# Attention in a planned order, with seven products for the queries and keys of two groups

## The chip, the cores and the metric

The kernel runs on one core of a Trainium2 chip. A core has a matrix engine (TensorE, PE in the profile, with its weight loads as PEld), three engines for elementwise work (VectorE or DVE, ScalarE or ACT, GpSimd or POOL), a queue that issues loads (SyncE or SP) and 16 DMA engines. The on-chip memory has 128 partitions; TensorE writes its sums into eight banks of a second memory, PSUM. The metric is the device time of one execution in microseconds (us).

## The reference, cut to what matters

Two transformer layers over 512 tokens of width 1024, all in float32. Layer 0 mixes the tokens with a gated recurrence, layer 1 with attention; each is followed by a gated feed-forward of width 2816. A conditioning vector gives, through a large matrix (`ada_w`), six vectors per layer that scale, shift and gate. The change lies mostly in the attention of layer 1:

```python
proj = (u @ w_in).reshape(B, S, N_GROUPS, 3, ATT_HEADS, ATT_HEAD_DIM)     # 512 x (3 groups x 3 x 8 heads x 128)
for gi, (window, dilation) in enumerate(((128, 1), (512, 4), (2048, 16))):
    q = apply_partial_rope(proj[:, :, gi, 0], cos, sin) * scale
    k = apply_partial_rope(proj[:, :, gi, 1], cos, sin)
    v = proj[:, :, gi, 2]
    o_g, lse_g = dilated_group_attention(q, k, v, window, dilation)
wts = softmax(stack(lses), axis=0)
o = einsum('gbsh,gbshd->bshd', wts, stack(outs))
y = o.reshape(B, S, D_MODEL) @ w_out
```

So there are 24 query/key pairs (8 heads in 3 groups), each a 1024 x 256 matrix against the 512 tokens.

## The kernel before, in words

**Three products for one.** To keep float32 precision, every operand of a matrix product is split into a high part (a copy on ScalarE into a reduced type) and a low part (the difference, a subtraction on VectorE). A product is then three matmuls: high by high, high by low, low by high (`three`, lines 437 to 440). One block of 128 output columns over a depth of 1024 is 8 x 3 = 24 matmuls with 512 tokens streaming (`block`).

**Seven products for eight.** In the feed-forwards' first products and in the values of groups 2 and 3 a 2 x 2 split of both matrices (Strassen's scheme, in Winograd's form) is used: seven half-size products take the place of eight, at the price of sums of the operands and of the results (`seven_products`, matmuls at line 853; `seven_values`, lines 1383 to 1466). The sums of the tokens' quarters are made once (`token_sums`, lines 748 to 770), the sums of the weights' quarters for each weight piece, in place in the raw buffer, and some of the products' sums by copying one PSUM bank into another as its start.

**Weights as a stream.** `Stream` (lines 38 to 135) holds one list of items in order of use: weight pieces of 1 MB ("w"), pieces for the seven products ("quarters", "half"), pieces of the conditioning matrix ("ada"), its closing steps ("do", "rows"). Two raw buffers alternate; the SyncE queue fills them. `take` hands out split pieces and, with a lead of two, has the next ones split in advance: line 88 copies the high part, line 89 subtracts the low part (whole pieces of 2048 columns), lines 108 and 109 do it in halves. There are three buffers for split pieces. A conditioning piece is four multiply-adds on VectorE (lines 257, 259); after two of them GpSimd sums over partitions (line 261), and small steps on VectorE turn the row into columns or add it to a gate (lines 271, 306).

**Attention.** The normalised tokens are copied into the order of the dilated groups (`apart`, lines 1676 and 1677). After the values of group 1 a loop runs over `order`: pairs of query and key, with the seven-product values of groups 2 and 3 for heads 0 to 3 near the start and for heads 4 to 7 in the middle. Each pair is two blocks of 24 matmuls, evacuated by ScalarE (lines 1704, 1705), with the rotary part turned on VectorE and copied back on ScalarE (lines 1712 to 1722). After each block `fl.tick()` lets one step of an earlier head follow: scores with masks and maxima (lines 1743 to 1775), the weights between groups (`merge_r`, `merge_n`: lines 1782 to 1805), transposes (1810 to 1817) and the sums over values (1836 to 1849). In this loop the build's scheduler sets the order on each engine. Everywhere that `tc.manual_schedule` stands, the order in the code is kept on TensorE, ScalarE, VectorE and GpSimd.

**After the loop.** `mixer_out` multiplies the eight heads' outputs by the output weights, one head per step `kt`, in manual order; the last steps of heads 6 and 7 stand between them in `tail`. Heads' outputs are split by `cut` (lines 434, 435), three of them first. Weights are taken at the first and the fifth step:

```python
for kt in range(3):
    cut(kt)
for kt in range(KT):
    if kt % 4 == 0:
        w = st.take(0)
    ...
    for t in range(NT):
        prods(y0[t], t, kt, w)
```

**The feed-forward of layer 0, second product.** Eleven weight pieces, each for two blocks of 128 of the inner width; `part` splits these blocks (lines 434, 435) two ahead. Conditioning pieces for layer 1 are woven between the weight pieces.

Of the kernel before, what the change touches and what calls it, by code (L numbers as in the profile page):

```python
# [1 line left out]

# [13 lines left out]
P = 128  # L16
# [21 lines left out]
class Stream:  # L38
# [73 lines left out]
    def whole(self):  # L112

        assert self.items[self.done][0] in WHOLE
        self.fill()
        self.done += 1
        return self.raw.pop(self.done - 1)
# [10 lines left out]
    def take(self, ahead=None):  # L128
# [7 lines left out]
        return self.ready.pop(0)  # L136

# [21 lines left out]
def block_kernel(tc, x, c, positions, ada_w, ada_b, norm_g, hgrn_w_in, lower, hgrn_norm_g, hgrn_w_out,  # L159
# [8 lines left out]
    with ExitStack() as ctx:  # L168
# [95 lines left out]
        def ada_item(l, v, hf, kq):  # L264
            src = ada_w[l, kq * 512:(kq + 1) * 512, v * D + hf * 512:v * D + (hf + 1) * 512]
            return ("ada", src.rearrange("(k p) n -> p k n", p=P), ada_chunk(l, v, hf, kq))
# [43 lines left out]
        def fin_item(l, v, hf):  # L310
            if v not in (2, 5):
                return ("do", None, col_fin(l, v, hf))
# [3 lines left out]
            return ("rows", (b, n), row_fin(l, v, hf))  # L316
# [62 lines left out]
        items += weave(f0b[:9], ada_seq((1, 1), (1, 0)), 0, 0.9) + f0b[9:]  # L379
# [4 lines left out]

        def aqk(g, hd):
            return ("w", tuple(AW[:, (g * 3 + k) * D + hd * P:(g * 3 + k) * D + (hd + 1) * P].rearrange(
                "(k p) n -> p k n", p=P) for k in range(2)))
# [23 lines left out]
        late = ada_seq((1, 2), (1, 4), (1, 3))  # L411
# [3 lines left out]
        woven(late[:8], 1.5)  # L415
# [4 lines left out]
        woven(late[8:], 1.3)  # L420
# [16 lines left out]
        def three(ps, ah, al, bh, bl, start, stop):  # L437
            pe.matmul(ps, ah, bh, start=start, stop=False)  # L438
            pe.matmul(ps, ah, bl, start=False, stop=False)  # L439
            pe.matmul(ps, al, bh, start=False, stop=stop)  # L440
# [942 lines left out]
        def seven_values(dsts, apart, th, tl):  # L1383


            C = lambda raw, c: V4(raw)[:, :, c * 256:c * 256 + 256]
            G = lambda t, o: V4(t[:, o * 1024:(o + 1) * 1024])
            u_of = lambda r, c: lambda kt, n: [a[:, r * 4 + kt, c * 256 + n * P:c * 256 + (n + 1) * P] for a in apart]
            t_of = lambda i: lambda kt, n: [a[:, i, kt, n * P:(n + 1) * P] for a in (th, tl)]
            raws, tiles = {}, {}  # L1390

            def cut(i, tile, o, k, c):
                hi, lo = tiles[i, tile]
                src = C(raws[i][k], c)
                act.copy(G(hi, o), src)
                dve.tensor_sub(G(lo, o), src, G(hi, o).bitcast(F32))

            def place(i, tile):
                tiles[i, tile] = st.part_tiles(V0)

            def prepare(i, step):
                if i >= len(dsts):
                    return
                if step == 0:
                    raws[i] = [st.whole(), st.whole()]
                    place(i, 0)
                    cut(i, 0, 0, 0, 0)
                    cut(i, 0, 1, 1, 1)
                elif step == 1:
                    place(i, 1)  # L1410
                    cut(i, 1, 0, 1, 0)
                    a, b = raws[i]
                    dve.tensor_add(C(b, 1), C(b, 1), C(a, 1))
                    dve.tensor_add(C(a, 1), C(a, 1), C(a, 0))
                    dve.tensor_add(C(a, 0), C(a, 0), C(b, 1))
                    dve.tensor_add(C(b, 0), C(b, 0), C(a, 0))
                    cut(i, 1, 1, 0, 0)
                elif step == 2:
                    place(i, 2)
                    cut(i, 2, 1, 0, 1)  # L1420
                    st.fill(1)
                    cut(i, 2, 0, 1, 1)
                else:
                    place(i, 3)
                    cut(i, 3, 0, 1, 0)
                    raws.pop(i)
                    st.fill()

            def run(ps, i, tile, o, us):
                hi, lo = tiles[i, tile]  # L1430
                for n in range(2):
                    for kt in range(4):
                        w = slice(o * 1024 + kt * 256, o * 1024 + (kt + 1) * 256)
                        three(ps[:, n * 256:(n + 1) * 256], *us(kt, n), hi[:, w], lo[:, w], kt == 0, kt == 3)

            H2 = lambda a: a.rearrange("p (n c) -> p n c", n=2)
            for step in range(3):
                prepare(0, step)
            for i, dst in enumerate(dsts):
                X, Y, Z, U = (dst[:, t:t + 2, c:c + 256] for c in (0, 256) for t in (0, 2))  # L1440
                m1 = bank("mm")
                run(m1, i, 0, 0, u_of(0, 0))
                act.copy(X, H2(m1))
                m4 = bank("a")
                run(m4, i, 0, 1, t_of(2))
                prepare(i, 3)
                m2 = bank("mm")
# [404 lines left out]
        for kind, g, i in order:  # L1852
            if kind == "v":
                if g == 1:

                    for fn in fl.at.pop(fl.n, []):
                        fn()
# [17 lines left out]
            for k in range(2):  # L1875
                ps = block(whi, wlo, k * D, P, u=apart)
                heads[i]["qk"[k], g] = qk_evac(ps, g, k, pair)
                if k == 1:
                    turn_pair(g, pair)
# [39 lines left out]
```

## Time and profile before

| what | value |
|---|---|
| median of 3 runs | 1510.54 us (1510.5 to 1513.27) |
| the profiled execution | 1511.44 us, span 1509.4 us |
| granted TensorE clock, mean | 0.997 |
| TensorE busy | 1493.7 us, 99% |
| VectorE busy | 1040.2 us, 69% |
| ScalarE busy | 746.6 us, 49% |
| GpSimd busy | 199.0 us, 13% |
| HBM | 192.31 MB read, 131 GB/s over the span |

The span is the time from the first to the last instruction that the profiler recorded; the execution's own time has some 2 us around it. Busy times are unions of an engine's instructions; matmuls overlap in their pipelines, so TensorE's progress is read better from the distance between the starts of matmuls than from the duration of one (0.39 us for 512 columns, while they start 0.227 us apart). In a group's row stand line, engine, operation, the names of output and inputs, sizes and count; then busy time and the mean of one in ns; then the engine's idle time before them and what ended it. In a row of the timeline the first two numbers are start and duration in us, and a bracket tells the idle time before it and what ended that.

### The profile page before, as it was taken

The numbers are of one execution on the slowest core, as the hardware profiler recorded it, in microseconds if no ns is written. First come the engines' busy times: TensorE is split into PE (matmuls) and PEld (weight loads), VectorE is DVE, ScalarE is ACT, GpSimd is POOL, SyncE is SP. The second block draws the span as 40 slices with busy tenths as digits, with TensorE's granted clock in tenths as the row PEclk, the third lists the DMA queues.
The fourth block names the chain that finished last, engine by engine and source line by source line (L and its number), as shares of the span: only waits on it lengthen the run. The fifth ranks groups of instructions, "written<-read, shape, count | busy, mean of one in ns | idle before, by whom it ended". The sixth has DMA issues, their size and how long they took to land. (4 is left out here: it accounts for less than half of the span.)

```text
span 1509.4 us, 23492 instructions
## 1 busy us (share of the span) xinstructions
PE 1493.7 (99%) x9231; PEld 1309.7 (87%) x9231; DVE 1040.2 (69%) x1807; ACT 746.6 (49%) x1321; POOL 199.0 (13%) x174
## 2 busy tenths in 40 slices
PE   8999999999999999999999999999999999999998
PEld 6777888898999988888988888988888899999886
DVE  4587768486888876577668766686466978887533
ACT  4443433362555542376546666356655555555231
POOL 1011211030111101040001110011002211110100
PEclk9999999999999999999999999999999999999999
DMA  9553444125333356424166540365213333334531
GB/s 309 166 183 126 156 152 168 56 85 167 101 109 107 107 200 213 155 108 141 57 183 191 151 120 29 123 185 141 84 52 117 100 97 112 112 112 141 199 108 56
DMA packets 206942, 199.14 MB, mean 132 GB/s; under 512 B 6840, under 2 KB 164720, under 8 KB 206576
## 3 DMA queue, kind: packets, MB, share of 16 engines
q1 hardware_dynamic: 203856, 190.87, 40.3%
q10 hardware_dynamic: 1952, 6.65, 1.2%
q8 instruction: 72, 1.18, 0.3%
q0 software_dynamic: 1024, 0.13, 0.2%
q14 instruction: 38, 0.31, 0.1%
HBM read 192.31 MB, written 5.31 MB: 131 GB/s over the span
## 5 line engine op out<-in xcount | busy, mean ns | idle before, releaser
L88 ACT CAST hi<-raw 128x2048 fp32r<-128x2048 f32 x68 | 129.7, 1907 | 199.1 <-DMA raw<-in_ffn_w_out_dram 60.8
L89 DVE TENSOR_TENSOR lo<-raw,hi 128x2048 fp32r<-128x2048 f32 x68 | 161.5, 2377 | 96.2 <-ACT hi L88 96.2
L438 PE MATMUL ps_mm<-apart,hi 128*128 128x512 f32 x384 | 151.4, 394 | 0.0
L439 PE MATMUL ps_mm<-apart,hi 128*128 128x512 f32 x384 | 151.2, 394 | 0.0
L440 PE MATMUL ps_mm<-apart,lo 128*128 128x512 f32 x384 | 150.6, 393 | 0.0
L438 PE MATMUL ps_mm<-uh,hi 128*128 128x512 f32 (+1 forms) x400 | 146.3, 366 | 0.0
L439 PE MATMUL ps_mm<-ul,hi 128*128 128x512 f32 (+1 forms) x400 | 144.3, 361 | 1.0 <-DVE ul L538 1.0
L440 PE MATMUL ps_mm<-uh,lo 128*128 128x512 f32 (+1 forms) x400 | 144.6, 361 | 0.0
L438 PE MATMUL ps_mm<-hi,oh 128*128 128x512 f32 x240 | 94.0, 392 | 0.0
L853 PE MATMUL ps_mm<-th,hiq 128*128 128x256 f32 x340 | 93.9, 276 | 0.0
L853 PE MATMUL ps_mm<-tl,hiq 128*128 128x256 f32 x340 | 93.9, 276 | 0.0
L853 PE MATMUL ps_mm<-th,loq 128*128 128x256 f32 x340 | 93.9, 276 | 0.0
L439 PE MATMUL ps_mm<-lo,oh 128*128 128x512 f32 x240 | 93.4, 389 | 0.0
L438 PEld LDWEIGHTS ps_mm<-uh,hi 128*128 128x128 f32 x400 | 75.5, 189 | 19.7 <-issue 8.4
L844 DVE TENSOR_TENSOR loq<-raw,hiq 128x1024 fp32r<-128x1024 f32 x68 | 80.2, 1221 | 16.8 <-ACT hiq L840 16.8
L439 PEld LDWEIGHTS ps_mm<-ul,hi 128*128 128x128 f32 x400 | 75.6, 189 | 12.1 <-DVE ul L538 1.4
L440 PEld LDWEIGHTS ps_mm<-uh,lo 128*128 128x128 f32 x400 | 75.5, 189 | 11.4
L824 POOL TENSOR_TENSOR raw<-raw 128x512 f32<-128x512 f32 x34 | 45.1, 1328 | 305.1 <-DVE spare L820 131.3
L440 PEld LDWEIGHTS ps_mm<-apart,lo 128*128 128x128 f32 x384 | 72.2, 188 | 14.5
L439 PEld LDWEIGHTS ps_mm<-apart,hi 128*128 128x128 f32 x384 | 72.2, 188 | 14.2
L438 PEld LDWEIGHTS ps_mm<-apart,hi 128*128 128x128 f32 x384 | 72.2, 188 | 14.1
L259 DVE SCALAR_TENSOR_TENSOR shared<-raw,cond,shared 128x512 f32<-128x512 f32 x98 | 73.2, 747 | 12.9 <-DMA raw<-in_ada_w_dram 11.9
(440 smaller groups left out, 4183.5 us busy)
## 6 DMA issues: line engine op xcount, KB each, us to landing
raw<-in_ada_w_dram SPq DMA_DIRECT2D x40, 1024.0 KB, 5.1
raw<-in_ffn_w_in_dram SPq DMA_DIRECT2D x136, 256.0 KB, 3.6
raw<-in_attn_w_in_dram SPq DMA_DIRECT2D x48, 512.0 KB, 5.1
raw<-in_ffn_w_out_dram SPq DMA_DIRECT2D x22, 1024.0 KB, 4.9
raw<-in_hgrn_w_in_dram SPq DMA_DIRECT2D x12, 1024.0 KB, 5.4
raw<-in_attn_w_in_dram SPq DMA_DIRECT2D x12, 1024.0 KB, 4.9
raw<-in_ffn_w_in_dram SPq DMA_DIRECT2D x10, 1024.0 KB, 5.0
first<-in_ada_w_dram SPq DMA_DIRECT2D x14, 512.0 KB, 7.9
```

The costliest lines, as they stand in the source:

```text
L88: self.nc.scalar.copy(hi, t)
L89: self.nc.vector.tensor_sub(lo, t, hi.bitcast(F32))
L259: dve.scalar_tensor_tensor(a, r[:, k], sc, a, op0=OP.mult, op1=OP.add)
L438: pe.matmul(ps, ah, bh, start=start, stop=False)
L439: pe.matmul(ps, ah, bl, start=False, stop=False)
L440: pe.matmul(ps, al, bh, start=False, stop=stop)
L824: pool.tensor_add(r[:, 2], r[:, 2], r[:, 0])
L844: dve.tensor_sub(lo, src, hi.bitcast(F32))
L853: pe.matmul(ps, w[x][:, a], us[kt][y], start=begin and kt + m == 0, stop=kt == 3 and m == 2, skip_group_check=True)
```

## The change

It has five parts.

1. The pairs of groups 2 and 3 are made by seven products. Their items become "quarters": four loads of 256 KB instead of two of 512 KB. `sevens` makes for each pair seven parts in two split buffers (three 512-wide pieces of the first, then all four of the summed raw buffer in two 1024-wide pieces), with four additions between, and seven products of 12 matmuls with 256 columns. Sums of products are made by copies of PSUM banks (`urgent`) and two additions for the keys. Pairs of group 1 stay as they are, except that the split is made in two halves.
2. All work of the loop is written down as tasks with an engine, an estimated duration, and names that they read and write. `Plan.run` lets these tasks run in a model at build time: each engine takes the ready task with the earliest due time, waits for a task marked urgent that is soon ready, and a task made by `EITHER` goes to VectorE or GpSimd, whichever is free first. The order found is written out as manual order on the four engines. The steps of the loop prepare their weights three steps ahead.
3. The scaling of the probabilities of groups 2 and 3 goes from VectorE (line 1798) to ScalarE.
4. Conditioning vector (1, 4), four pieces and two closing steps, moves from the attention loop to the second product of the feed-forward of layer 0, where twelve pieces are now woven in instead of eight.
5. In that product the low parts of the inner blocks are subtracted on GpSimd instead of VectorE.

`mixer_out` and its `tail` are not touched; the plan hands the stream back with `st.done = heads_end`, the first item of the output weights.

```diff
-        items += weave(f0b[:9], ada_seq((1, 1), (1, 0)), 0, 0.9) + f0b[9:]
+        items += weave(f0b, ada_seq((1, 1), (1, 0), (1, 4)), 0, 0.69)
...
+        by_seven = lambda g: g > 0
...
-        late = ada_seq((1, 2), (1, 4), (1, 3))
+        late = ada_seq((1, 2), (1, 3))
...
-                    split(oh, ol, mid(f))
+                    act.copy(oh, mid(f))
+                    (pool if l == 0 else dve).tensor_sub(ol, mid(f), oh.bitcast(F32))
...
+        def EITHER(n, fn, r=(), w=()):
+            plan.add("DVE", (n + 80) / 960, lambda e: fn(pool if e == "POOL" else dve), r, w, other=("POOL", n * 0.0027 + 0.1))
...
+        def sevens(g, hd):
+            def cut(part, k):
+                ACT(0.58, lambda: act.copy(Q(p.t[0], part), Q(raw.t, k)), ...)
+                EITHER(512, lambda e: e.tensor_sub(Q(p.t[1], part), Q(raw.t, k), Q(p.t[0], part).bitcast(F32)), ...)
+            def add(to, k):
+                EITHER(512, lambda e: e.tensor_add(Q(raw.t, to), Q(raw.t, to), Q(raw.t, k)), [raw(k)], [raw(to)])
+            def prepare_1():
+                cut(0, 1,)
+                add(1, 0,)
+                cut(1, 1,)
+                add(0, 2,)
+                add(1, 2,)
+                cut(2, 1,)
+                add(1, 3,)
+            def prepare_2():
+                for n in range(2):
+                    ACT(1.0, lambda two=two: act.copy(p.t[0][:, two], raw.t[:, two]), ...)
+                    EITHER(1024, lambda e, two=two: e.tensor_sub(p.t[1][:, two], raw.t[:, two], p.t[0][:, two].bitcast(F32)), ...)
+            def products_1():
+                run(first, 0, 0, a_of(0, 0), True)
+                ACT(0.36, lambda: act.copy(u2.t[:, lo], first.t[:, lo]), [first()], [u2()], urgent=True)
+                run(both, 0, 1, T3, True)
+                ACT(0.36, lambda: act.copy(xs.t[:, lo], both.t[:, lo]), [both()], [xs(0)])
+                run(u2, 0, 2, t2, False)
+                ACT(0.36, lambda: act.copy(u4.t[:, lo], u2.t[:, lo]), [u2()], [u4()], urgent=True)
+            def products_2():
+                run(first, 1, 3, a_of(1, 0), False)
+                queries(first, 0)
+                run(u4, 1, 0, t1, False)
+                ACT(0.36, lambda: act.copy(xs.t[:, hi], u4.t[:, lo]), [u4()], [xs(1)], urgent=True)
+                run(u2, 1, 2, T4, False)
+                keys(1, 1, both)
+                keys(0, 0, u2)
+                run(u4, 1, 1, a_of(1, 1), False)
+                queries(u4, 1)
+                turned(g, rows, q, k)
...
+        with tc.manual_schedule(engines=ORDERED):
+            planned = plan.run()
+        st.done, st.taken = heads_end, st.taken + sum(k == "qk" and not by_seven(g) for k, g, _ in order)
```

More of the change, by code (lines that the diff above doesn't have):

```diff
@@ L1 @@
 from contextlib import ExitStack
+import heapq
 import numpy as np
@@ new lines, in next_weights, with split_place, products, go @@
+        def next_weights():
+            while True:
+                item = st.items[at_item[0]]
+                at_item[0] += 1
+                if item[0] in ("w", "quarters", "half"):
+                    return queue.pop(0)
+                condition(item)
+        def split_place(first):
+            return plan.place("hl", 3, lambda: st.part_tiles(first))
+        def products(cost, dst, key, terms, begin, reads):
+            def go():
+                todo = [p for t in terms() for p in t]
+                for i, (x, y) in enumerate(todo):
+                    pe.matmul(dst(), x, y, start=begin and i == 0, stop=i == len(todo) - 1, skip_group_check=True)
+            PE(cost, go, reads, [key])
@@ L1873, in block_kernel @@
[L1873 to L1881 removed]
+                steps += [("v", None, None, k, *p) for k, p in enumerate(value_unit(g - 1, i))]
+            else:
+                two = sevens(g, i) if by_seven(g) else plain(g, i)
+                steps += [("qk", g, i, k, *p) for k, p in enumerate(two)]
```

649 lines of the change are left out of this document (537 added, 112 removed).

## The prediction

> **What bounds the kernel now.** I read the page from the top: the span, the busy shares, the slices.
>
> ```profile
> span 1509.4 us, 23492 instructions
> PE 1493.7 (99%) x9231; PEld 1309.7 (87%) x9231; DVE 1040.2 (69%) x1807; ACT 746.6 (49%) x1321; POOL 199.0 (13%) x174
> PE   8999999999999999999999999999999999999998
> PEclk9999999999999999999999999999999999999999
> ```
>
> TensorE (PE) is busy in every slice at the full granted clock, so only fewer or shorter matmuls, or a new wait, can move the time. A busy PE is not yet a PE at its peak, so next comes the spacing of matmuls, from the view of busy time by stretches (columns: stretch, length, then per engine the busy time and the instructions; granted clock, DMA share, GB/s).
>
> ```profile
> core 0: us, PE busy (x) PEld busy (x) DVE busy (x) ACT busy (x) POOL busy (x), PEclk, DMA share, GB/s
> 14.00:20.00 6.00, 5.00 (x21) 3.85 (x22) 5.72 (x13) 4.20 (x10) 1.79 (x2) 0.62 1.15 316
> 400.00:520.00 120.00, 120.00 (x1052) 120.00 (x1051) 96.86 (x99) 69.85 (x114) 15.51 (x12) 1.00 0.38 110
> 560.00:640.00 80.00, 80.00 (x354) 66.25 (x353) 47.69 (x80) 24.79 (x23) 10.07 (x3) 1.00 0.56 190
> 705.00:1105.00 400.00, 398.84 (x2277) 349.16 (x2277) 265.49 (x689) 227.51 (x446) 40.21 (x36) 1.00 0.43 127
> 953.00:981.00 28.00, 28.00 (x238) 28.00 (x237) 18.35 (x19) 8.78 (x9) 0.00 (x0) 1.00 0.36 115
> ```
>
> At 560 to 640 only matmuls of 512 columns run: 80/353 = 0.2266 us each. At 400 to 520 the feed-forward's seven-product stage runs with 256 columns: 120/1051 = 0.1142 us. The seven-product values at 953 to 981, 256 columns too, need 28/237 = 0.118 us. Attention's loop is 705 to 1105, and PE is idle there for 1.2 us in 400.
>
> **The seven products (A).** A query/key pair of groups 2, 3 is now 2 blocks x 8 x 3 = 48 matmuls of 512 columns, 48 x 0.2266 = 10.88 us. It becomes 7 products x 4 x 3 = 84 of 256 columns: 84 x 0.1142 = 9.59 us, or 9.91 us at the values' spacing. All of it lies on the path. There are 8 heads x 2 groups = 16 pairs, so it saves 16 x 1.29 = 20.6 us, or 16 x 0.97 = 15.5 us at the worse end. I take 20.6: the new products stream the tokens past stationary weights, as those at 400 to 520 do, where the values stream the weights.
>
> **What the splits cost (B).** Per pair, a 2048-wide split goes. New are three 512 and two 1024 copies on ScalarE, as many subtractions and four 512 additions, each on VectorE or GpSimd by the plan; four 256-wide seeds and copies more on ScalarE; two key additions on VectorE.
>
> ```profile
> L89 DVE TENSOR_TENSOR lo<-raw,hi 128x2048 fp32r<-128x2048 f32 x25 | 58.8, 2352 | 33.5 <-ACT hi L88 33.5
> L88 ACT CAST hi<-raw 128x2048 fp32r<-128x2048 f32 x24 | 45.8, 1906 | 60.8 <-DMA raw<-in_attn_w_in_dram 31.9 <-PE ps_mm L439 22.6 <-PE ps_mm L440 6.3
> L844 DVE TENSOR_TENSOR loq<-raw,hiq 128x1024 fp32r<-128x1024 f32 x68 | 80.2, 1221 | 16.8 <-ACT hiq L840 16.8
> L832 DVE TENSOR_TENSOR raw<-raw 128x512 f32<-128x512 f32 x34 | 23.5, 691 | 1.1
> L861 DVE TENSOR_TENSOR shared<-shared,ps_mm 128x256 f32<-128x256 f32 x34 | 14.0, 413 | 0.0
> L840 ACT CAST hiq<-raw 128x1024 fp32r<-128x1024 f32 x68 | 68.0, 1047 | 17.4 <-DVE raw L828 16.6 <-DVE raw L832 0.8
> L434 ACT CAST oh<-mid 128x512 fp32r<-128x512 f32 x44 | 26.2, 619 | 62.3 <-PE ps_b L439 47.7 <-PE ps_mm L439 10.4 <-DVE shared L259 1.4
> L857 ACT ACTIVATE shared<-ps_mm 128x256 f32<-128x256 f32 x34 | 13.1, 384 | 1.6
> L1798 DVE TENSOR_SCALAR h<-h,wE 128x256 f32<-128x256 f32 x28 | 8.3, 356 | 0.2
> L259 DVE SCALAR_TENSOR_TENSOR shared<-raw,cond,shared 128x512 f32<-128x512 f32 x42 | 31.4, 747 | 6.8 <-DMA raw<-in_ada_w_dram 6.4
> ```
>
> VectorE per pair: 7 x 0.691 + 2 x 1.221 + 2 x 0.413 = 8.1 us in place of 2.35. Over 16 pairs that is +92 us; the four conditioning loads that leave this loop take back 16 x 0.747 = 12 us, the row scaling that goes to ScalarE 8 us. So 265.5 + 92 - 20 = 337 us of 379 us, 89%, before GpSimd helps. ScalarE per pair: 3 x 0.619 + 2 x 1.047 + 4 x 0.384 = 5.5 us in place of 1.9, evacuations about even: 227.5 + 16 x 3.6 + about 10 for the row scaling = 295 us, 78%. Neither passes PE, so all of it is covered as long as each part is ready in time. A pair's chain is three rounds of copy, subtraction, addition, 3 x (0.62 + 0.69 + 0.69) = 6 us on VectorE, against some 12 us between two pairs on PE (a 9.6 us pair and a third of a head's scores and sums).
>
> **GpSimd beside VectorE (C).** The plan counts on both at once. What the trace shows of that:
>
> ```profile
> 405.04 1.29 POOL L824 TENSOR_TENSOR raw<-raw 128x512 f32<-128x512 f32 x1 [8.38 <-DVE loq L820]
> 405.15 0.41 DVE L861 TENSOR_TENSOR shared<-shared,ps_mm 128x256 f32<-128x256 f32 x1
> 405.67 1.21 DVE L862 SCALAR_TENSOR_TENSOR mid<-shared 128x512 f32<-128x512 f32 x1
> L862 DVE SCALAR_TENSOR_TENSOR mid<-shared x34: 682/1209/1216, 396.0 to 1389.3; 128x512 f32<-128x512 f32 x34
> ```
>
> The operation of line 862 takes 0.68 us at best and 1.21 us beside GpSimd's; the one that reads PSUM beside SBUF (line 861) stays at 0.41. [...] By the row: 16 x 9 + 4 x 11 + some 14 operations = 202 may go to either; with a third on GpSimd, 67 x 0.53 = 35 us are lost and about 63 of 190 us are saved, so VectorE stands at 337 - 63 + 35 = 309 us, 82%. The seven-product stage has VectorE at 96.86 of 120 us, 81%, and PE at 120.00 of 120. So I take 2 us for PE waits inside the loop: nearest to that row. The ends are 0 and 17.5 us (half of the 35, if every second delay reaches PE through ScalarE's queue: a copy that waits for its addition holds up the seeds behind it, for which PE waits). Below 0 it can't go, as only 1.2 us of idle time are there.
>
> **Start and values (D).** Group 2's products of head 0 now need the token sums one pair earlier, and the second half-matrix of the values waits for a buffer that the pair before holds longer. In the trace of before no PE wait stands there. Ends: 0, and one DMA landing of 5.1 us (row below); I take 2 us.
>
> **The end of the loop (E).** Now the first two pieces of the output weights are split while the last pairs run. In the plan nobody splits them: the taking of weights inside the output product does it, at its first and fifth step, behind what ScalarE and VectorE have in order there.
>
> ```profile
> raw<-in_attn_w_in_dram SPq DMA_DIRECT2D x48, 512.0 KB, 5.1
> 1105.13 0.76 ACT L1704 ACTIVATE shared<-ps_mm 32x256 f32<-32x256 f32 x2 [1.67 <-PE ps_mm L440]
> 1106.53 1.66 ACT L434 CAST oh<-oT 128x512 fp32r<-128x512 f32 x3
> 1107.39 0.47 PE L438 MATMUL ps_mm<-hi,oh 128*128 128x512 f32 x1
> 1108.10 1.09 ACT L1838 COPY oT_late<-ps_b 128x512 f32<-128x512 f32 x1
> 1108.97 0.64 ACT L1815 COPY h<-ps_a 128x512 f32<-128x512 f32 x1
> 1109.51 1.67 ACT L1722 COPY qk<-shared 32x256 f32<-32x256 f32 x4
> 1110.33 1.06 PE L1761 MATMUL ps_a<-qk,qk 128*128 128x128 f32 x8
> 1121.85 0.39 PE L438 MATMUL ps_mm<-hi,oh 128*128 128x512 f32 x1
> 1123.31 0.16 DVE L1782 TENSOR_TENSOR wM<-sN,oN 128x4 f32<-128x4 f32 x1
> 1124.89 1.08 DVE L1805 TENSOR_SCALAR h<-h,wE 128x128 f32<-128x128 f32 x4
> ```
>
> First step: from 1105.13, evacuation 0.76, three cuts 1.66, then the new copy 1.91 and subtraction 2.35: 1111.8. PE has sums and transposes until 1107.39 and 0.9 us of scores (eight matmuls at the row of 1110.33), to 1108.3, so it waits 3.5 us. If the plan's own copies (1.09 + 0.64 + 1.67 us in this trace) go ahead of the cuts, 7 us. Fifth step: PE wants the second piece at 1121.85; its subtraction stands behind the merge that ends at 1124.89 + 1.08 = 1125.97, and ends at 1128.3: 6.4 us. Ends: 0 (the scheduler moves the splits up, as it has before) and 13.4; I take 3.5 + 6.4 = 9.9, as the trace has the cuts ahead of those copies.
>
> **Feed-forward of layer 0 (F).** Four more conditioning loads come between the eleven weight loads of the output product, and 22 subtractions of 0.69 us go to GpSimd.
>
> ```profile
> 556.89 0.37 SPq L68 DMA_DIRECT2D raw<-in_ffn_w_out_dram  x1
> 562.99 1.91 ACT L88 CAST hi<-raw 128x2048 fp32r<-128x2048 f32 x1 [5.11 <-DMA raw<-in_ffn_w_out_dram]
> 564.93 2.29 DVE L89 TENSOR_TENSOR lo<-raw,hi 128x2048 fp32r<-128x2048 f32 x1 [2.89 <-ACT hi L88]
> 567.25 0.37 SPq L68 DMA_DIRECT2D raw<-in_ffn_w_out_dram  x1
> ```
>
> A weight's round, from its load's issue to the next issue into that buffer, is 10.4 us, and PE uses one up in 48 x 0.2266 = 10.9 us. An extra load between two weights adds its four operations, 3 us: 13.4 against 10.9, 2.5 us lost four times, mostly won back where one load stands between (0.5 us) and from three pieces of lead. Ends 0 and 10; I take 1.5, nearer to none, since the window 560 to 640 shows PE full. The subtractions on GpSimd are done a weight ahead (10.9 us): nothing, if their queue isn't held by a partition sum; 3 us, one such sum, if it is.
>
> **Sum.** -20.6 + 2 + 2 + 9.9 + 1.5 = -5.2 us. The profiled execution took 1511.44 us (span 1509.4 and 2.0 around it), 0.9 over the median of 1510.54; from the median: 1505.3, so 1505.
>
> **Rivals.**
> 1. It ends slower: the plan's order breaks on GpSimd. If the loss of 0.53 us for each of 67 operations reaches PE every second time (C's upper end), 2 becomes 17.5: 1505 + 15.5 = 1521. It decides from about 8 us of such waits. For it: ScalarE's queue is strict and three quarters full. Against: the stage at 400 to 520.
> 2. The gaps at the end cost clock too. The row at 14 to 20 has a granted clock of 0.62 behind short idle times, 6 x 0.38 = 2.3 us lost; twice that, and E at 13.4, gives 1505 + 4.6 + 3.5 = 1513. [...]
> 3. The change doesn't do all it says: the new products run at 0.118 us, as the values do. Then A is 15.5: 1510.
> 4. The gain comes whole: the scheduler hides E and F is covered: -20.6 + 4 = -16.6, 1494.
>
> **How the numbers follow.** This forecast 0.28, rival 4 0.22, rival 1 0.20, rival 2 0.20, rival 3 0.10. About 0.2%, 3 us, is what a measurement can tell here. Faster: 0.28 + 0.22 = 0.50. Same: rival 3 and a fifth of rival 2, 0.14. Slower: the rest, 0.36. The range goes from 1490 (rival 4 with the best ends of C and D) to 1522 (rival 1); the forecast's own is 1499 to 1509.
>
> **What would show it.** A: 84 matmuls per pair, 0.114 us apart, in the stretch of the pairs. B, C: VectorE near 80% and additions beside GpSimd at 1.2 us. D: a PE gap ahead of the first values. E: two PE gaps of 3 to 7 us after the last pair, ended by the low part of the output weights. F: PE gaps in the output product of layer 0 ended by such a subtraction. I am wrong if PE waits for seeds inside the pairs, in many small gaps, or if E isn't there.

## The result, and the profile after

The changed kernel took 1659.78 us (median of 4 runs, 1658.09 to 1664.36) against 1510.52 us before: a ratio of 1.0988, 95% interval 1.0962 to 1.1015. I had forecast 1505 with a range to 1522. The direction is wrong, and the time lies 138 us outside the range.

The page of the changed kernel:

```profile
span 1659.4 us, 25186 instructions
PE 1526.7 (92%) x9807; PEld 1356.7 (82%) x9807; DVE 1142.6 (69%) x1854; ACT 799.3 (48%) x1484; POOL 373.7 (23%) x266
PE   8999999999999987899879677888888999999998
PEclk9999999999999989899889889999998999999999
```

Apart from the first and the last slice, which are the same before, TensorE has idle time from the middle of the first feed-forward to the end of attention's loop, and nowhere else; the granted clock falls in seven of these slices. GpSimd's busy time has nearly doubled and is still only 23%: its busy share says nothing here. The two stages in the view by stretches, after and then before (same columns as in the prediction):

```profile
570.00:690.00 120.00, 98.10 (x386) 78.20 (x385) 63.52 (x112) 31.90 (x45) 42.12 (x27) 0.89 0.45 158
690.00:1250.00 560.00, 469.38 (x3120) 431.79 (x3119) 400.61 (x792) 319.50 (x676) 187.85 (x120) 0.93 0.31 93
```

```profile
570.00:690.00 120.00, 120.00 (x546) 99.45 (x545) 80.01 (x132) 60.61 (x94) 27.62 (x24) 1.00 0.45 155
690.00:1115.00 425.00, 423.84 (x2414) 370.70 (x2413) 281.46 (x723) 239.61 (x464) 40.30 (x36) 1.00 0.42 125
```

In the same 120 us of the first feed-forward TensorE gets through 386 matmuls in place of 546: 160 x 0.2266 = 36 us are missing. ScalarE and VectorE are less busy than before, so neither is what is short. What everybody waits for is named by GpSimd's timeline there (start, length, line, operation, count, and in brackets the idle time before it and its releaser):

```profile
580.15 3.25 POOL L394 PARTITION_ALL_REDUCE shared<-shared  x1 [5.96 <-issue]
590.25 3.77 POOL L1092 TENSOR_TENSOR ol<-mid,oh 128x512 fp32r<-128x512 f32 x3 [6.85 <-issue]
600.04 3.25 POOL L394 PARTITION_ALL_REDUCE shared<-shared  x1 [6.02 <-issue]
610.45 2.52 POOL L1092 TENSOR_TENSOR ol<-mid,oh 128x512 fp32r<-128x512 f32 x2 [7.16 <-issue]
618.74 3.25 POOL L394 PARTITION_ALL_REDUCE shared<-shared  x1 [5.77 <-issue]
629.22 4.18 POOL L1092 TENSOR_TENSOR ol<-mid,oh 128x512 fp32r<-128x512 f32 x3 [7.23 <-issue]
```

Read the brackets. In these rows, where a partition sum follows a subtraction, GpSimd stands still for 5.8 to 6.0 us; where a subtraction follows a sum, for 6.9 to 7.2 us. The releaser is "issue": it waits for nothing that the profile shows. Rows of the views of lines 394 (the sums) and 1092 (the subtractions) have what GpSimd's queue did at these places (count, shortest, median and longest in ns, first and last start in us):

```profile
L394 POOLq MODIFY_POOL_CONFIG  x10: 2/4/12, 574.4 to 652.2; - x10
L1092 POOLq MODIFY_POOL_CONFIG  x12: 98/98/98, 562.1 to 660.9; - x12
```

So a turn of one sum and two or three subtractions costs 3.25 + 6 + 7 + 2.5 to 4 = 19 to 20 us, of which 6 or 7 are counted as busy. The instructions in the two rows take 98 ns or less each; what fills the idle time beside them isn't shown. The waits of the stage, for all engines (waiter, what it waits for: us in total, times, longest):

```profile
POOL ol L1092 <- issue: 35.3, 5, 7.2
DVE diag L404 <- POOL shared L394: 28.1, 5, 6.8
POOL shared L394 <- issue: 23.5, 4, 6.0
PE ps_mm L576 <- POOL ol L1092: 10.6, 2, 8.4
PE ps_mm L575 <- DVE lo L90: 9.8, 3, 4.5
```

TensorE is hit twice: by the late subtractions themselves (line 576), and by VectorE, which waits in line 404 for the late sum while the next weight's low part (line 90) is queued behind. The loop has the same: its costliest gap, from GpSimd's timeline and TensorE's:

```profile
943.48 3.25 POOL L1970 PARTITION_ALL_REDUCE shared<-shared  x1 [5.87 <-issue]
953.56 1.25 POOL L2047 TENSOR_TENSOR loq<-raw,hiq 128x512 fp32r<-128x512 f32 x1 [6.84 <-issue]
...
954.87 0.58 PE L2008 MATMUL ps_mm<-apart,loq 128*128 128x256 f32 x1 [14.85 <-POOL loq L2047]
```

From 937.6, when GpSimd ends the transfer ahead of this sum, to 954.8 it does 4.5 us of work, and TensorE waits 14.85 us for one low part, its longest wait in the loop.

### The profile page after: what moved, and what is told of

It reads as the page before. It is cut to its first block, busy times and chain, and to the rows that moved or that the text cites. A ratio compares the mean times of both kernels' runs of the same rounds, so it can differ in the third digit from the quotient of the medians.

```text
span 1659.4 us, 25186 instructions
## 1 busy us (share of the span) xinstructions
PE 1526.7 (92%) x9807; PEld 1356.7 (82%) x9807; DVE 1142.6 (69%) x1854; ACT 799.3 (48%) x1484; POOL 373.7 (23%) x266
## 3 DMA queue, kind: packets, MB, share of 16 engines
q0 software_dynamic: 1024, 0.13, 0.2%
## 5 line engine op out<-in xcount | busy, mean ns | idle before, releaser
L89 ACT CAST hi<-raw 128x2048 fp32r<-128x2048 f32 x45 | 85.8, 1906 | 175.6 <-DMA raw<-in_ffn_w_out_dram 99.3
L2008 PE MATMUL ps_mm<-apart,hiq 128*128 128x256 f32 (+1 forms) x608 | 148.8, 338 | 10.9 <-ACT xs L2114 8.4
L90 DVE TENSOR_TENSOR lo<-raw,hi 128x2048 fp32r<-128x2048 f32 x45 | 105.3, 2343 | 52.8 <-ACT hi L89 52.8
L2008 PEld LDWEIGHTS ps_mm<-apart,hiq 128*128 128x128 f32 x608 | 105.3, 199 | 20.4 <-ACT xs L2114 9.0
L2008 PE MATMUL ps_mm<-apart,loq 128*128 128x256 f32 (+1 forms) x304 | 101.1, 332 | 19.1 <-POOL loq L2047 14.9
L575 PE MATMUL ps_mm<-lo,oh 128*128 128x512 f32 x240 | 98.0, 408 | 11.7 <-DVE lo L90 11.7
L2008 PE MATMUL ps_mm<-uh,hiq 128*128 128x256 f32 x256 | 77.6, 303 | 23.1 <-ACT ps_mm L2093 10.7
L2008 PE MATMUL ps_mm<-uh,loq 128*128 128x256 f32 x256 | 75.7, 296 | 13.0 <-POOL loq L2047 12.1
L576 PE MATMUL ps_mm<-hi,ol 128*128 128x512 f32 x176 | 71.2, 405 | 10.6 <-POOL ol L1092 10.6
L2008 PEld LDWEIGHTS ps_mm<-apart,loq 128*128 128x128 f32 x304 | 60.6, 199 | 24.8 <-POOL loq L2047 15.1
```

The lines of the kernel that those rows point to most:

```text
L89: self.nc.scalar.copy(hi, t)
L90: self.nc.vector.tensor_sub(lo, t, hi.bitcast(F32))
L575: pe.matmul(ps, ah, bl, start=False, stop=False, skip_group_check=part)
L576: pe.matmul(ps, al, bh, start=False, stop=stop, skip_group_check=part)
L2008: pe.matmul(dst(), x, y, start=begin and i == 0, stop=i == len(todo) - 1, skip_group_check=True)
```

## The experiments

The median of the kernel before moved between 1510.5 and 1514.0 us from one series of runs to the next, so differences between series are good to some 3 us. Theory S: switching GpSimd between its two kinds of work. Theory P: contention with VectorE. Theory V: too much vector work with seven products in any case.

**The first feed-forward's subtractions back on VectorE**

```diff
-                    (pool if l == 0 else dve).tensor_sub(ol, mid(f), oh.bitcast(F32))
+                    dve.tensor_sub(ol, mid(f), oh.bitcast(F32))
```

> One edit to the changed kernel: the 22 subtractions of the first feed-forward's output go back to VectorE; the four added conditioning loads stay where the change put them, and the loop's GpSimd work stays. Theory S (GpSimd pays about 6 us before a partition sum that follows a subtraction and about 7 us before a subtraction that follows a partition sum): the switches in this stage go, and with them most of the 34 us that TensorE waits between 570 and 690 us; 1659.8 - 34 = about 1626, 1615 to 1640. Theory P (GpSimd and VectorE contend, the switch is only an idle wait): only 22 subtractions of about 1.4 us beside VectorE's are lifted, and VectorE gets 22 more of about 0.65 us; 1650 to 1660. Theory V (the vector work of the added loads is what is too much here): the loads stay, VectorE gets more, and it is slower than 1660.

1630.9 us (ratio to before 1.0775, 1.0758 to 1.0793): 28.9 us less. Theory S's number. The stage has 535 matmuls in its 120 us:

```profile
570.00:690.00 120.00, 118.22 (x535) 97.09 (x534) 92.84 (x165) 59.52 (x93) 32.57 (x26) 1.00 0.55 184
```

VectorE has more to do (92.8 us) and TensorE waits less, which rules V out here.

**The loop's operations on VectorE**

```diff
-            plan.add("DVE", (n + 80) / 960, lambda e: ..., r, w, other=("POOL", n * 0.0027 + 0.1))
+            plan.add("DVE", (n + 80) / 960, lambda e: ..., r, w)
```

> One edit to the changed kernel: in the plan every low part and every sum of weights is VectorE's, none GpSimd's; GpSimd keeps the partition sums and the small DMAs. The stage of the first feed-forward stays as the change has it. Theories S and P: of the 500 us from 745 to 1245 (403 before; seven products should take off about 17) most of some 110 us comes back, and VectorE gets about 60 operations of 0.6 to 1.1 us more, of which some show: 1550 to 1580. Theory V (the loop with seven products asks too much of ScalarE and VectorE, with GpSimd or without): VectorE goes from 352 us to about 410 of 400 to 500, and the time stays at 1620 or more.

1550.6 us (1.0244, 1.0226 to 1.0261): 109.2 us less. V falls for the loop too.

**Both**

> Both edits at once: GpSimd does no subtraction in either stage. Theories S and P: the sum of the two gains, 1515 to 1550; what is left over the kernel before is about 10 us at the end of the loop (the output weights' splits) less 17 us of seven products plus what VectorE now makes late. Theory V: 1620 or more.

1519.1 us (1.0042, 1.0025 to 1.0059): 140.7 us less, the sum of the two (138.1) within the error. With no subtraction on GpSimd the rest of the change is 0.4% slower than before. Both kernels run the same 9807 matmuls, but TensorE's busy time falls from 1526.7 to 1482.7 us:

```profile
PE 1482.7 (98%) x9807; PEld 1325.0 (87%) x9807; DVE 1128.8 (74%) x1946; ACT 800.6 (53%) x1484; POOL 198.2 (13%) x174
```

44 of the 141 us were therefore matmuls drawn out; the other 97 are idle time. The mean granted clock of the two executions, 0.964 and 0.993, fits the 44: 1526.7 x 0.964 and 1482.7 x 0.993 are both 1472 us.

**No partition sums where GpSimd subtracts**

```diff
-                if kq == 1:
+                if kq == 1 and (l, v) not in ((1, 0), (1, 1), (1, 4)):
                     pool.partition_all_reduce(a, a, P, ...)
...
-                if kq[0] == 1:
+                if False:
                     POOL(3.3, lambda: pool.partition_all_reduce(...), w=[a()])
```

> The changed kernel without the partition sums of layer 1's conditioning in the first feed-forward and in the loop (that part of the computation is left out: the sums over partitions of vectors 0 to 4 are not made); every subtraction stays on GpSimd as the change has it. Nothing switches any more there, and the contention of GpSimd's subtractions with VectorE stays in full. Theory S: about 34 us of the first feed-forward and the greater part of the loop's 110 come back, 1530 to 1580. Theory P: only the sums' own 3.25 us each and their idle are saved, and the time stays above 1620. Theory V: above 1640.

1594.2 us (1.0535, 1.0511 to 1.056): 65.6 us less, between the two forecasts. Switching (with the 10 sums themselves, which this kernel leaves out) is 65.6 us: about 29 in the feed-forward and 37 in the loop. For the feed-forward four kernels show it, by the first and the last start of one kind of its matmuls: with subtractions and sums on GpSimd, with the subtractions alone (this run), with the sums alone (the first experiment), and with neither (a run further down):

```profile
L574 PE MATMUL ps_b<-hi,oh x44: 388/389/632, 539.4 to 693.1; 128*128 128x512 f32 x44
L574 PE MATMUL ps_b<-hi,oh x44: 389/389/389, 536.6 to 661.5; 128*128 128x512 f32 x44
L574 PE MATMUL ps_b<-hi,oh x44: 389/389/395, 536.6 to 657.0; 128*128 128x512 f32 x44
L574 PE MATMUL ps_b<-hi,oh x44: 389/389/389, 537.1 to 656.5; 128*128 128x512 f32 x44
```

These are 153.7, 124.9, 120.4 and 119.4 us. The sums alone cost 1 us, the subtractions alone 5.5, both together 34.3: some 28 us are the alternation. The other 75.1 us, up to the kernel with everything on VectorE, are not switching. So neither theory was enough. VectorE's groups in the loop, first with all on VectorE, then here (count, then busy us and mean ns):

```profile
L2181 DVE TENSOR_TENSOR loq<-raw,hiq 128x1024 fp32r<-128x1024 f32 x28 | 33.4, 1219 | 5.1 <-ACT hiq L2180 5.1
L2185 DVE TENSOR_TENSOR raw<-raw,raw 128x1024 f32<-128x1024 f32 x12 | 14.7, 1223 | 0.3
L2294 DVE CUSTOM_DVE_ANT_0 h<-ps_a,maskR 128x128 f32<-128x128 f32 x60 | 14.5, 285 | 4.7 <-PE ps_a L2291 4.7
```

```profile
L2181 DVE TENSOR_TENSOR loq<-raw,hiq 128x1024 fp32r<-128x1024 f32 x14 | 23.6, 1688 | 17.6 <-ACT hiq L2180 17.6
L2185 DVE TENSOR_TENSOR raw<-raw,raw 128x1024 f32<-128x1024 f32 x11 | 19.2, 1749 | 0.7
L2294 DVE CUSTOM_DVE_ANT_0 h<-ps_a,maskR 128x128 f32<-128x128 f32 x60 | 14.2, 285 | 3.3 <-PE ps_a L2291 3.3
```

These two groups with two inputs in SBUF go from 1.22 to 1.7 us in the mean (line 2047 from 0.69 to 0.85); the one that reads PSUM stays at 0.285. That contention is there is shown; what it costs is not, yet.

**The kernel before, with the feed-forward's subtractions on GpSimd**

```diff
-                    split(oh, ol, mid(f))
+                    act.copy(oh, mid(f))
+                    (pool if l == 0 else dve).tensor_sub(ol, mid(f), oh.bitcast(F32))
```

> The kernel before with one edit: the low parts of the first feed-forward's output (22 subtractions) go to GpSimd, between the four partition sums of that stage, which begin at 552, 571, 589 and 609 us. Theory S (each sum between subtractions takes GpSimd 3.25 + 6 + 7 us, and subtractions behind it come late): four such turns, at 4 to 6 us of TensorE's time each, 1513 + 16 to 24 = 1525 to 1540. Theory P (only contention with VectorE): 1512 to 1520.

1526.0 us (1.0075, 1.0058 to 1.0093): 12.4 us more than before (1513.6 in this series), the low end of S. The same two idle times appear in a kernel without plan, moved loads or new products:

```profile
577.46 3.25 POOL L261 PARTITION_ALL_REDUCE shared<-shared  x1 [5.81 <-issue]
588.28 6.33 POOL L956 TENSOR_TENSOR ol<-mid,oh 128x512 fp32r<-128x512 f32 x4 [7.57 <-issue]
```

With four sums it costs 3 us a sum; with the change's six in this stage, nearly 5.

**The softmax's small transfers from another queue**

```diff
-                POOL(0.85, lambda: pool.dma_start(scr[hd, 0]..., sN.t), ...
+                STAT(0.85, lambda: nc.sync.dma_start(scr[hd, 0]..., sN.t), ...     # the other three alike
```

> The changed kernel without the partition sums of layer 1's conditioning in the first feed-forward and in the loop (left out as in the run without sums, 1594.2), and with the four small transfers of the softmax's maxima and sums per head issued from SyncE's queue in place of GpSimd's; the subtractions stay on GpSimd. Theory Q (what is left of the loss there comes of GpSimd's queue: a subtraction stands behind a transfer that waits for ScalarE's exponentials or for a landing, 29 to 56 us in sum): 1545 to 1575. Theory P (it comes of GpSimd's and VectorE's slower operations beside each other, 1.2 us becoming 1.7 to 2.2): 1585 to 1600.

1585.5 us (1.0477, 1.0461 to 1.0493): 8.7 us less than without sums. GpSimd's transfers ahead of its subtractions are a small part; theory Q falls.

**Contention alone, in two doses**

```diff
+        spare, owed = fresh(ap, [P, 171], "spare", 1), [0.0]
+        flat = [a.rearrange("p k n -> p (k n)")[:, 0:171].bitcast(F32) for a in apart]
         def EITHER(n, fn, r=(), w=()):
-            plan.add("DVE", (n + 80) / 960, lambda e: ..., r, w, other=("POOL", n * 0.0027 + 0.1))
+            plan.add("DVE", (n + 80) / 960, lambda e: fn(dve), r, w)
+            owed[0] += 0.36 * n / 512          # second kernel: 0.2
+            while owed[0] >= 1:
+                owed[0] -= 1
+                plan.add("POOL", 1.4, lambda e: [pool.tensor_sub(spare, flat[0], flat[1]) for _ in range(3)], r)
```

> As the kernel whose subtractions are all VectorE's (1519.1), without the partition sums of layer 1's conditioning (left out as before), and with subtractions on GpSimd in the loop that nobody needs: 315 of 128x171 elements, as much as GpSimd did there in the run without sums (about 137 us of its time), put beside VectorE's own and written to a tile that nothing reads. Nothing waits for them but GpSimd's own small transfers. Theory P (the two engines slow each other down where both work from SBUF): VectorE's operations of 1.2 us go to 1.6 or more while GpSimd works, its 341 us in the loop become 380 or more, and the time 1535 to 1565. Theory R (what was left of the loss without sums, 75 us, comes of waiting for GpSimd's results, each twice as long as VectorE's and in a fixed order): 1517 to 1530.

> The run with unneeded GpSimd subtractions in the loop (1570.6, where they took 250 us of GpSimd's time rather than the 137 aimed at, 813 ns each) with 175 of them in place of 315, so that GpSimd's time is about 140 us, as it was with its real subtractions and no sums. The same sums are left out. Theory P in proportion: 1519 + 52 x 140/250 = 1548, 1540 to 1556, and then some 46 of the 75 us that were left without sums are not contention but waits for GpSimd's results and queue. If contention is all of the 75: 1585 or more. If it only begins near saturation of VectorE: under 1530.

1570.6 us (1.0376, 1.0353 to 1.0398) with the full dose and 1539.4 us (1.0176, 1.0161 to 1.0192) with the smaller one. GpSimd's time on them, in the two kernels:

```profile
L1936 POOL TENSOR_TENSOR spare<-apart,apart 128x171 f32<-128x171 f32 x307 | 249.7, 813 | 23.2
```

```profile
L1936 POOL TENSOR_TENSOR spare<-apart,apart 128x171 f32<-128x171 f32 x174 | 161.6, 929 | 15.5 <-DVE apart L1729 2.9
```

VectorE needs 405 us for the 826 operations that took 355 for 824 with GpSimd quiet (stretches of the full dose, then of the kernel with all on VectorE):

```profile
690.00:1165.00 475.00, 430.16 (x2995) 394.69 (x2994) 405.13 (x826) 294.30 (x636) 279.33 (x346) 0.97 0.34 101
```

```profile
690.00:1115.00 425.00, 412.67 (x2995) 387.56 (x2994) 354.57 (x824) 292.92 (x627) 33.14 (x34) 0.99 0.38 113
```

So work that nobody needs costs 20.3 us at 162 us of GpSimd's time, and 51.5 us at 250: more than in proportion; delays to GpSimd's small transfers, which stand in the same queue, were not separated from it. The 162 hold 15.2 us of the first of these operations alone, which begins ahead of the stretch, so the smaller dose is rather 146. The real operations without sums took 137 us of GpSimd (67 of them); in proportion to the smaller dose that is 17 to 19. Contention is 17 to 20 of the 75 us, an estimate: the doses are many short operations, the real ones few long ones, and no kernel has everything on VectorE with the sums left out, to which the doses should be compared. How unevenly the doses ran is in the view of their line (shortest, median and longest in ns, full dose):

```profile
L1936 POOL TENSOR_TENSOR spare<-apart,apart x315: 544/615/15200, 677.6 to 1138.1; 128x171 f32<-128x171 f32 x158
```

**The same plan, carried out by VectorE**

```diff
-            plan.add("DVE", (n + 80) / 960, lambda e: fn(pool if e == "POOL" else dve), r, w, other=...)
+            plan.add("DVE", (n + 80) / 960, lambda e: fn(dve), r, w, other=...)
```

> The run without sums (1594.2; layer 1's partition sums left out), with the plan made as there, GpSimd's operations at GpSimd's price and place, but carried out by VectorE in the loop, where the plan's order puts them. Theory O (the fixed order, written for two engines, is what the engines wait in): 1560 or more. Theory G (GpSimd's operations, twice as long as VectorE's, and what waits for them): the loop runs as with all on VectorE, 1517 to 1535.

1548.8 us (1.0244, 1.0227 to 1.0261), between the two forecasts: 45.4 us of the 75 come back when VectorE carries out GpSimd's share in the same order, and the other 29.7 only with an order made for VectorE alone. The division isn't clean, since here VectorE has more to do than the plan counted on; and the first feed-forward's subtractions are still GpSimd's here, so that about 5 of the 29.7 belong to that stage (the 124.9 us above against 120.4 and 119.4). Of the 45, contention is 17 to 20 and the transfers 9; the last 16 to 19, which would be the wait for results that take 2.4 to 2.8 us in place of 1.2, I have by subtraction only, and they stay open.

**A plan that knows the price of a switch**

```diff
-                    POOL(3.3, lambda: pool.partition_all_reduce(...), w=[a()])
+                    POOL(16.5, lambda: pool.partition_all_reduce(...), w=[a()])
```

> The run with the feed-forward's subtractions on VectorE and the loop as changed (1630.9), with the plan's price of a partition sum raised from 3.3 to 16.5 us (the sum, some 6 us before it and some 7 behind it), so that the plan gives GpSimd less beside the sums and orders what waits. If the loop's loss by switching (36 us: the 112 between this run and the one without GpSimd's subtractions, less the 75) came of the wrong price: 1595 to 1610. If it comes of GpSimd's time itself, which no order gives back: 1620 to 1635.

1601.4 us (1.0587, 1.0571 to 1.0603), against 1630.9 with the plan's own price: 29.5 us go when one number in the plan is right. The sums are still made and the idle times beside them still stand. Not all of the 29.5 is switching, though: with the higher price the plan also gives GpSimd less, 55 operations of 114 us in the loop in place of 70 of 142 us. At the 45 us for 137 of the run above, that would be 9 of the 29.5, an estimate.

**The seven products undone**

```diff
-        by_seven = lambda g: g > 0
+        by_seven = lambda g: False
```

> On top of the same edit (1519.1): the queries and keys of groups 2 and 3 by plain products again, 48 of 0.227 us per pair in place of 84, so that the plan's order and the moved loads are alone. Theory A (the spacing of 0.1165 us is what a new product costs; 16 pairs save 16 x 1.1): 1519 + 17.5 = 1537, 1533 to 1540. Rival V (what the seven products save is lost again in waits for their more numerous casts, copies and subtractions): 1510 to 1525.

1532.3 us (1.012, 1.0106 to 1.0134), with all operations on VectorE: the seven products are worth 13.2 us. It also shows what the plan costs without them: 18.7 us over before in this series (1513.6), of which the next experiment finds 10 at the loop's end. The other 8 or so are the price of the plan's order and the moved loads together, which the seven products more than pay for. In the kernel with them (everything on VectorE) they run at 0.118 us each, as the values do: the first and the last of 24 in a row,

```profile
1040.12 0.28 PE L2008 MATMUL ps_mm<-uh,hiq 128*128 128x256 f32 x1
...
1042.83 0.28 PE L2008 MATMUL ps_mm<-uh,loq 128*128 128x256 f32 x1
```

(1042.83 - 1040.12) / 23 = 0.118.

**The output weights split inside the plan**

```diff
+        for _ in range(2):
+            raw, p = queue.pop(0), plan.place("hl", 3, lambda: st.part_tiles(0))
+            for n in range(2):
+                ACT(1.0, cast, [raw()], [p("h", n)], goal=clock[0] - 4.0)        # act.copy of one half
+                DVE(1.15, rest, [raw(), p("h", n)], [p("l", n)], goal=clock[0] - 4.0)
+            done_with_raw()
+            out_w.append(p)
         with tc.manual_schedule(engines=ORDERED):
             planned = plan.run()
+        for p in out_w:
+            st.raw.pop(heads_end + len(st.ready))
+            st.ready.append(p.t)
-        st.done, st.taken = heads_end, ...
+        st.done, st.taken = heads_end + 2, ...
```

> On top of the edit that takes GpSimd's subtractions away in both stages (1519.1): the first two chunks of the output weights are split inside the plan (ScalarE and VectorE, four halves of each), with the raw tile freed and the next load started from there. Theory E (the first output product waits for a split that starts only when the plan has ended; the gaps of 4.8, 2.3, 4.2 and 2.4 us between 1099 and 1129 us of that kernel): they close, 1519 - 11 = about 1508, 1506 to 1511. Rival (VectorE, busy 341 of 400 us in the loop, has no room, so the splits push the last heads): 1514 to 1520.

1508.9 us (7 runs, ratio to before 0.9976, 0.9964 to 0.9988), 10.2 us less than 1519.1. These two waits, at the end of the loop in the kernel without the splits, are what it took away:

```profile
PE ps_mm L574 <- ACT hi L89: 8.3, 2, 4.5
PE ps_mm L575 <- DVE lo L90: 3.1, 2, 1.6
```

This is the fastest of all: the change without GpSimd's subtractions and with these splits beats both kernels, though before only by 0.24% (0.12 to 0.36).

**The moved loads: back, and more of them.** On that kernel, the four loads of the change go back into the loop; or the four of another vector go the same way.

```diff
-        items += weave(f0b, ada_seq((1, 1), (1, 0), (1, 4)), 0, 0.69)
+        items += weave(f0b[:9], ada_seq((1, 1), (1, 0)), 0, 0.9) + f0b[9:]              # back
+        items += weave(f0b, ada_seq((1, 1), (1, 0), (1, 4), (1, 3)), 0, 0.53)           # more
```

> On top of the kernel with the output weights split inside the plan (1508.9): the four conditioning loads that the change moved into the first feed-forward go back to the loop, where the kernel before has them. Theory F (with VectorE alone the feed-forward pays for them: a gap of 2.2 us at 622 us and a slower clock behind it, some 4 us in all, and the loop has room): 1503 to 1507. Rival (22 more operations of 0.3 to 0.75 us in a loop whose VectorE is busy 341 of 400 us cost as much there): 1508 to 1515.

> On top of the kernel with the output weights split inside the plan (1508.9): the four loads of one more conditioning vector of layer 1 go from the loop to the first feed-forward's output. Putting four loads back into the loop had cost 15 us, with VectorE at 89% from 800 to 1000 us. Theory L (VectorE's load in the loop is what a load costs): the loop gains 5 to 12, the feed-forward, whose VectorE goes from 75% of 560 to 640 us to some 90%, pays 2 to 6: 1499 to 1506. Rival (the feed-forward's output, with its loads at 67 to 69% of the DMA engines, becomes the place that waits): 1508 to 1520.

Back: 1523.6 us (1.0069, 1.0052 to 1.0085), 14.8 more. More: 1526.4 us (1.0093, 1.0077 to 1.0109), 17.6 more. Both are worse than either theory had. Back in the loop, the loads' 16 operations of 0.75 us and some short ones, about 14 us of VectorE's work, cost 14.8. But taking four more out gains nothing there. The pairs' products, first and last start in the loop, with the change's loads, with four back, and with four more taken out:

```profile
L2008 PE MATMUL ps_mm<-apart,hiq x608: 276/281/478, 717.2 to 1098.0; 128*128 128x256 f32 x96, 128*128 128x512 f32 x56
L2008 PE MATMUL ps_mm<-apart,hiq x608: 276/281/496, 714.2 to 1109.9; 128*128 128x256 f32 x96, 128*128 128x512 f32 x56
L2008 PE MATMUL ps_mm<-apart,hiq x608: 276/281/478, 734.2 to 1117.2; 128*128 128x256 f32 x96, 128*128 128x512 f32 x56
```

These are 380.8, 395.7 and 383.0 us: more work on VectorE made the loop longer, and less didn't make it shorter. (The loads that went back also bring two partition sums and their use of a raw buffer; no run separates these.) In the feed-forward the twelve loads of the change are near what it carried: with them TensorE waits 1.8 us between 560 and 660 us; with sixteen, it waits six times for a weight's high part and six times for a low part, 13 us in all, because the load came late.

```profile
ACT hi L89 <- DMA raw<-in_ffn_w_out_dram: 36.0, 8, 6.8
PE ps_mm L574 <- ACT hi L89: 8.0, 6, 2.0
PE ps_mm L575 <- DVE lo L90: 5.0, 6, 2.1
```

## Why the prediction was wrong

Two steps failed, C and F, and it is GpSimd's help that both priced wrongly. The sum has 2 us for it in the loop and 1.5 us for the first feed-forward; taking it away gives back 109.2 and 28.9 us. Both leave out what GpSimd loses when it goes from a subtraction to a partition sum and back, 13 us a turn.

The 149 us by the runs: feed-forward switching 29, loop switching 37, GpSimd's carrying out its operations 45 (contention 17 to 20, transfers 9, the rest not separated), the order written for two engines 30 (about 5 of them in the first feed-forward), and 6 to 8 for the rest of the change: 10 lost at the loop's end, 2 to 4 won by everything else, the seven products' 13 included.

- **F failed by the price of a sum.** It priced a subtraction behind a partition sum at "3 us, one such sum, if it is" held, and 1.5 us for the whole stage. Measured: 3.25 + 13 us of GpSimd a turn, and 28.9 us. GpSimd's timeline of before has the sums of that stage 18 to 20 us apart, each behind idle time put down to ScalarE or VectorE; a switch would have been hidden in that. The queue's own row, below, was there to be read. I took the engine's idle time as time at its disposal and looked for no stage where sums and subtractions alternate. The moved loads were also mispriced the other way: in the loop they would have cost 14.8 us (measured with everything on VectorE), a gain that step F left out. The first of the sums of that stage in before, and the row of its queue:

```profile
552.47 3.26 POOL L261 PARTITION_ALL_REDUCE shared<-shared  x1 [16.14 <-ACT hi L88]
L261 POOLq MODIFY_POOL_CONFIG  x10: 7/17/37, 237.2 to 1367.4; - x10
```

- **C failed by its list of causes, and this is the larger part.** It had contention alone, between 0 and 17.5, and took 2. By the doses contention is 17 to 20, at its upper end and above: I relied on the seven-product stage, where VectorE is 81% busy with 12 operations of GpSimd, not 67. Missing altogether were switching (37), the order (30) and what else GpSimd's carrying out costs (25 to 28). The prediction took the 0.53 us of the row of line 862 as the loss of every operation. That one began 0.63 us after GpSimd's of 1.29, so only the last 0.66 us of GpSimd's lay beside it; what is lost beside one of 2.4 to 2.8 us, as in the loop, the row doesn't show. There the means of lines 2181 and 2185, two inputs in SBUF, rose from 1.22 to 1.7 us, and line 2294, which reads PSUM, stayed at 0.285. How much of the rise is waiting for the other engine isn't shown; in the full dose 250 us of GpSimd's work lengthened VectorE's by 50.
- **B was right,** and spoke against the change's use of GpSimd: VectorE was forecast at 89% of the loop without help and shows 354.6 of 425 us, 83%; ScalarE 78% and 69%. (VectorE's work added there: 72 us forecast, 73 shown.) With everything on VectorE, TensorE idles 11 of the loop's 418 us, from the last copy into `apart` to the first product of the output weights, against 1 of 423 before: the loop is 5 us shorter. The help was not needed.
- **A was mis-sized.** Taken 0.1142 us a product and 20.6 us, measured 0.118 and 13.2 (the worse end was 15.5). Rival 3 had the right spacing: that tokens stream past weights did not make these products like the feed-forward's.
- **D:** with all on VectorE TensorE waits no more than 1.3 us in one place between 690 and 800 us; the 2 us taken weren't visible as one gap.
- **E was right:** 9.9 forecast, 10.2 measured, at the two places named.
- **Rivals.** Rival 1 named the right engine and deciding event, waits on GpSimd in the plan's order, and a price seven times too small. Rival 2's lower clock behind gaps is in both stages of the result, not at the end alone: 0.89 and 0.93 granted, against 1.00 before; behind the wait of 14.85 us above it was 0.50 from 954.87 to 958.10 us, and 1.00 from 958.35 to 962. In all, 44 us of longer matmuls.

## What to carry to other kernels

GpSimd's idle time was not free time here (13 us of it went with every turn): before giving an engine a second kind of work, look for the place in a trace where it goes from the one to the other, and read the idle time before each. A planner is as good as its prices: one wrong number for GpSimd's sums cost up to 30 us. Measure first whether the helper is needed at all: here VectorE alone had room, and the only version faster than before does without GpSimd's help.

## What the runs showed of the hardware

- Where the profile names no releaser, GpSimd stood still 5.7 to 6.0 us before a partition sum that follows an elementwise operation (7.1 and 7.3 us at the first sum of the first feed-forward's second product), and 6.8 to 7.8 us on the way back, in the changed kernel, there at a MODIFY_POOL_CONFIG in its queue, and in the one before with a single edit.
- From the kernel with everything on VectorE to the one without sums, where GpSimd has its share, VectorE's operations with two SBUF inputs went from 1.22 to 1.75 us in the mean in line 2185 and to 1.69 in line 2181, but from 1.34 to 1.22 in line 2136; those of lines 2294 and 2109, which read PSUM, stayed at 0.285 and 0.416. GpSimd's 128x171 subtractions in the full dose took 0.544 us at the shortest, 0.615 in the median and 0.813 in the mean. They write one tile again and again; whether that plays a part wasn't tried.
